# One layer of three mixers on one core: the order of all instructions from a list scheduler in the kernel, in place of an order written part by part

## The chip, the cores and the metric

The kernel runs on one NeuronCore of a Trainium2 chip. TensorE (PE in the profile) does the matrix products, VectorE (DVE), ScalarE (ACT) and GpSimd (POOL) the rest; all transfers are issued by SyncE (SP), in order. Each engine takes its instructions in the order of the program and waits for the others by semaphores. The metric is the device time of one execution in microseconds, less is better; three timed runs stand for the kernel before.

## The reference, cut to what matters

1040 tokens (16 learned ones and 1024 of the input) of 1024 channels in float32. They are normalised, projected once to 7832 columns, and three groups of heads work on their columns; the 2048 channels that come out are projected to 1024, normalised and added to the input.

```
hn   = rms_norm(h, norm_pre)
proj = hn @ w_in                                    # 1024 -> 7832
mixed = concat([gated_deltanet(p_a),                # 6 heads of 128
                rwkv7(p_b),                         # 8 heads of 64
                mamba2(p_c)])                       # 12 heads of 64, 4 groups
h    = h + rms_norm(mixed @ w_out, norm_post)       # 2048 -> 1024
```

DeltaNet and RWKV-7 carry a state from token to token through a matrix that differs for each token. In chunks (128 tokens for DeltaNet here, 64 for RWKV-7) this is a triangular system per chunk, and a short recurrence over the chunks. Mamba-2 has a scalar decay, so its chunks need no system.

## The kernel before, in words

**Tiles and products.** Channels lie on partitions, tokens along the free axis. `w_in` is cut in 61 tiles of 128 columns. A projection of one tile (`proj`, `conv`, `shifted`; tile name `pj`) has three pieces of about 347 tokens; a piece is 24 products on the whole 128x128 array into one bank: 8 tiles of the depth times three passes, because operands are split in a rounded part and its rest (type float32r). All else on TensorE is in plain float32, which takes two passes each, and much of it on smaller tiles of the array: 32x32, 64x64, 64x128, 128x64.

**Units.** The work is cut in units, written as generators that yield between their parts. `unit_a` is one DeltaNet head (a0 to a5): it projects k; makes the matrix of each chunk (`agk`); sends its blocks of 32 through DRAM to one block per partition; solves them there on VectorE (`solve32`, tile `alb`); merges blocks 32 to 64 to 128 (`am`); and goes over nine chunks (`aks`, `av`, `ads`, `aops`), each product waiting for an element-wise step on the one before. `unit_b` is a pair of RWKV-7 heads (b0 to b3), with grams (`bgr`), a solve (`blb`), merges (`bm`) and 17 chunks (`bsi`, `bu`, `bd`). `unit_c` is half of Mamba-2 (c0, c1). `unit_o` is the output projection (tile `po`): half of the columns for eight token tiles, two of them (po0 and po1) at once at the start, then the other half. Its weights come through a ring of three raw buffers (`or`), its input (`omre`, `omrw`) from DRAM.

**What sets the order.** `schedule` (L1169) takes units in the order of `PLAN` and keeps a clock of TensorE's work. `Meter` (L79) adds up about how long a part takes on TensorE, and how long the way back over the other engines is. When the next part of a scan should be ready on that clock it is emitted whole, otherwise one product of a projection. Emission gives a priority (`high_priority` with `PRI`, `EVA`, `CALM`), and the framework's own scheduler sets the order on each engine by priority and dependence. More than two units may scan at once, sharing two lanes of banks.

## Time and profile before

| what | value |
|---|---|
| three timed runs | 1523.97, 1532.54, 1538.36 us; median 1532.54 |
| span of the profiled execution | 1518.0 us (its own time beside the span is not shown) |
| instructions in the profile | 25931 |
| busy share PE, DVE, ACT, POOL | 94%, 67%, 43%, 16% |
| mean granted clock of TensorE | 0.970 |
| set-up; mixed middle; output projection | 0 to 38; 38 to 1302; 1302 to 1518 us |

A product of matrices shows from its start to its modelled end and overlaps with the next, so the pace is read from start to start. A float32 product leaves two records, one for each pass, and some records of products are missing from the trace. The granted clock is 1.0 at 2.4 GHz and 0.5 at 1.2 GHz. Counts of products and of changes between them are taken from the order of the program, times from the trace.

### The profile page before, as it was taken

Reading aid. Unit: us, or ns where it says so; the run is one execution under the profiler, and the core shown is the slowest. Engines: PE = TensorE matmul, PEld = TensorE weight load, DVE = VectorE, ACT = ScalarE, POOL = GpSimd, SP = SyncE. Lnnn points to the kernel's source line nnn. Section 1 sums busy time; section 2 is a strip of 40 time slices with the busy share of each in tenths; the row PEclk is TensorE's granted clock in tenths of the full one; section 3 lists DMA queues with packets and bytes.
Section 4 is the critical chain, followed back from the end, with each engine's and each line's share of the span. In section 5 each row is a group of like instructions: output and inputs, shape, how many; then the busy total and the mean of one; then the engine's idle time right before and its main releaser. Section 6 shows DMA issues by size and latency. Waiting matters only on the chain.

```text
span 1518.0 us, 25931 instructions
## 1 busy us (share of the span) xinstructions
PE 1427.0 (94%) x9657; PEld 1259.6 (83%) x9657; DVE 1014.6 (67%) x2688; ACT 647.8 (43%) x1814; POOL 239.2 (16%) x227
## 2 busy tenths in 40 slices
PE   4999999999999999997999999999999999889897
...
GB/s 187 58 85 43 70 33 39 29 41 64 29 30 47 49 74 43 86 31 53 46 43 50 43 46 53 36 29 57 97 59 61 43 36 44 169 159 89 250 193 56
DMA packets 102880, 104.28 MB, mean 69 GB/s; under 512 B 37915, under 2 KB 70427, under 8 KB 102755
## 3 DMA queue, kind: packets, MB, share of 16 engines
...
## 4 chain that ended last, share of the span: by engine, by line
PE 30%; DVE 14%; issue 5%; ACT 4%; DMA 3%; POOL 0%; SPq 0%; DVEq 0%; ACTq 0%; POOLq 0%
PE pj L96 14%; PE po L96 5%; DVE s_tmp L96 3%; DVE alb L96 2%; PE am L96 2%; DMA or<-in_w_out_dram 2%; PE bsi L96 1%; DVE aq L181 1%; DMA omrw<-d_mix 1%; PE aops L96 1%; PE ads L96 1%; DVE av L181 1%; PE aks L96 1%; PE av L96 1%; ACT clt L904 1%
## 5 line engine op out<-in xcount | busy, mean ns | idle before, releaser
L96 PE MATMUL pj<-hh,w 128*128 128x350 f32 (+8 forms) x2928 | 773.9, 338 | 0.2 <-ACT hh L261 0.2
L96 PEld LDWEIGHTS pj<-hh,w 128*128 128x128 f32 x2928 | 516.7, 192 | 13.2 <-issue 2.1
L96 PE MATMUL pj<-hl,w 128*128 128x350 f32 (+8 forms) x1464 | 493.4, 337 | 0.0
L150 POOL TENSOR_TENSOR w<-wr,w 128x512 fp32r<-128x512 f32 x122 | 173.6, 1424 | 870.3 <-ACT w L149 631.7
L96 PEld LDWEIGHTS pj<-hl,w 128*128 128x128 f32 x1464 | 281.3, 192 | 6.6 <-issue 0.9
L149 ACT CAST w<-wr 128x512 fp32r<-128x512 f32 x122 | 74.9, 615 | 75.8 <-PE pj L96 64.4
L96 PE MATMUL po<-ow,omw 128*128 128x512 f32 x408 | 95.5, 395 | 6.2 <-ACT omw L1064 3.7
L96 PEld LDWEIGHTS po<-ow,omw 128*128 128x128 f32 x408 | 77.2, 190 | 24.6 <-ACT omw L1064 4.4
L96 PE MATMUL po<-ow,ome 128*128 128x512 f32 x360 | 90.6, 399 | 4.6 <-ACT ow L1046 1.8
L96 PEld LDWEIGHTS po<-ow,ome 128*128 128x128 f32 x360 | 66.6, 188 | 20.1 <-POOL ow L1047 2.5
...
L96 DVE TENSOR_TENSOR buv<-bu,b_ib 64x128 f32<-64x128 f32 x68 | 19.1, 281 | 69.5 <-PE bu L96 69.3
...
L96 PEld LDWEIGHTS bsi<-buv,bgm 64*64 64x64 f32 (+1 forms) x528 | 42.1, 139 | 17.5 <-issue 2.2
L828 ACT COPY by<-bsi 64x128 f32<-64x128 f32 x64 | 16.7, 262 | 82.3 <-PE bsi L96 81.8
L181 DVE SCALAR_TENSOR_TENSOR cbc<-pj,pack,cbc 128x346 f32<-128x346 f32 (+4 forms) x72 | 40.5, 568 | 14.3 <-ACT cbc L178 13.5
...
L96 PE MATMUL bgr<-bar,bbk 64*128 64x128 f32 x272 | 43.8, 328 | 2.6 <-DVE bbk L96 2.0
L1065 DVE TENSOR_TENSOR ome<-omre,ome 128x512 fp32r<-128x512 f32 (+2 forms) x40 | 22.4, 594 | 34.1 <-ACT ome L1064 34.0
L1047 POOL TENSOR_TENSOR ow<-or,ow 128x512 fp32r<-128x512 f32 x16 | 21.0, 1316 | 135.9 <-ACT ow L1046 135.9
...
## 6 DMA issues: line engine op xcount, KB each, us to landing
wr<-in_wt_dram SPq DMA_DIRECT2D x122, 256.0 KB, 2.6
or<-in_w_out_dram SPq DMA_DIRECT2D x32, 256.0 KB, 2.6
omrw<-d_mix SPq DMA_DIRECT2D x32, 256.0 KB, 4.7
clt<-d_cs SPq DMA_DIRECT2D x24, 256.0 KB, 4.5
omre<-d_mix SPq DMA_DIRECT2D x24, 256.0 KB, 4.2
...
```

The source lines that it names most:

```text
L96: return op(out, *args, **kw)
L149: nc.scalar.copy(w[:, 0], raw)
L150: nc.gpsimd.tensor_tensor(w[:, 1], raw, w[:, 0].bitcast(F32), SUB)
L181: nc.vector.scalar_tensor_tensor(acc[:, a + z: b], p[:, o + z - s: o + b - a - s], cw[:, 3 - s: 4 - s], acc[:, a + z: b], MUL, ADD)
L828: nc.scalar.copy(yt[hs[(c - 1) % 2], (c - 1) // 2, :], pq[64:128, 0:128])
L904: nc.scalar.activation(t[:, e, i], t[:, e, i], AF.Exp, bias=self.ncs[:, 1 + 4 * w + i, k + e: k + e + 1])
L1047: (nc.vector if k % 2 else nc.gpsimd).tensor_tensor(t[:, 1], raw, t[:, 0].bitcast(F32), SUB)
L1065: nc.vector.tensor_tensor(t[:, 1], raw, t[:, 0].bitcast(F32), SUB)
```

## The change

The kernel's instructions stay as they are, and their order is set by the kernel itself. From `scalars` on, an engine call no longer emits: `write` records an `Instr` with the instructions it depends on (from the bytes that it reads and writes, and from buffers that come round again) and with a duration from a table. Each unit and each postponed projection is a `Task` with one queue per engine, so within a task an engine keeps the order of the source. The main loop takes, of all engines, the head that can start first by the table. On TensorE it keeps to projections until at least `BURST` (1.0 us) of them stand in a row, then takes scan parts in a round for as long as one is ready within `JOIN` (0.25 us), those of the bank that was last written first. On the other engines heads that are ready within 0.05 us are chosen by class (`LESS`). `emit` binds each instruction behind the one before on its engine, so the framework does not reorder. A lane of banks belongs to one unit at a time, so two units scan at once. `PLAN` is changed, and `Meter`, its constants and the waits that a part tells by its `yield` are gone.

```
-PLAN = "a0 b0 b1 b2 c0 b3 a1 a2 a3 c1 a4 a5"
+PLAN = "a0 b0 b1 a1 c0 b2 a2 c1 b3 a3 a4 a5"
-LOOK, LATE, EVAC, DMA = 0.05, 0.3, 2.0, 5.0
-PRI, EVA, CALM = 300, 700, 1500
+BURST, JOIN = 1.0, 0.25
+LESS = {"scan": 0.0, "ev": 0.3, "ld": 0.5, "calm": 1.0, "off": 0.4}
+AHEAD = 8
...
+            fast = name == "matmul" and args[0].dtype == F32R
+            i.mode = (r(rows), r(cols), fast)
+            i.step = (n / 2400 + 0.013 if fast else 0.109 if name == "transpose" else
+                      0.063 if r(cols) == 32 else 2 * max(0.058 if r(cols) == 64 else 0.112, n * 0.00085))
+            i.extra = {128: 0.165, 64: 0.108, 32: 0.07}[r(cols)]
+        elif key == "DVE":
+            i.step = 0.065 + n * (0.00116 if len(ins) > 2 else 0.00105)
+        elif key == "ACT":
+            i.step = 0.105 + 0.00078 * n if name == "copy" else 0.14 + 0.00086 * n
+        elif key == "POOL":
+            i.step = 0.04 + n * (0.0024 if name == "tensor_tensor" else 0.001)
+        else:
+            last = min(a.ap[-1][1] if a.ap[-1][0] == 1 else 1 for a in (out, args[0]))
+            total = int(np.prod(out.shape)) * 4
+            i.step, i.extra = 0.46, total / 380e3 * (1 if last >= 128 else 1.5 if last >= 32 else 4)
+        self.task.q[key].append(i)
...
+    def ready(self, i):
+
+        if i.start is None:
+            t = 0.0
+            for d in i.deps:
+                if d.done is None:
+                    return None
+                if not d.eng == i.eng == "PE":
+                    t = max(t, d.done + SEES[i.eng])
+            i.start = t
+        return i.start
+
+    def emit(self, i, start):
+        r = i.go()
+        ins, was = r.ins, self.before.get(i.eng)
+        if was is None:
+            self.tc.keep_in_program_order(r)
+        else:
+            self.tc.add_manual_dep(ins, was, mybir.DependencyInfo(mybir.DependencyClass.NoSync, mybir.DependencyReason.DATA), reason="order")
+        self.before[i.eng] = ins.name
+        if i.eng == "PE":
+            if self.array and self.array != i.mode:
+                if self.array[:2] != i.mode[:2]:
+                    start += 0.093
+                if i.mode[2] and not self.array[2]:
+                    i.step += 0.1
+            self.array = i.mode
+        self.free[i.eng] = start + i.step
+        if i.eng == "SP":
+            self.bus = max(self.bus, start + 0.4) + i.extra
+            i.done = max(start + 2.0, self.bus + 1.3)
+        else:
+            i.done = start + i.step + i.extra
+        i.start, i.go = start, None
+        i.deps = ()
+        i.task.q[i.eng].pop(0)
...
-            if ready and (when(ready[0]) <= self.clock + LOOK or not can):
-                s = ready[0]
-                self.clock = max(self.clock, when(s))
-                if s["lane"] is None:
-                    used = [sum(o["lane"] == g for o in active) for g in range(len(GB))]
-                    s["lane"] = used.index(min(used))
-                self.lane = s["lane"]
-                with self.tc.high_priority(CALM if s["calm"] else PRI):
-                    step(s)
...
+                    if s["on"] and not s["on"]["done"] or not safe(s):
+                        continue
+                    if s["lane"] is None:
+                        open_ = [g for g in range(len(GB)) if all(o["lane"] != g for o in active)]
+                        if not open_:
+                            continue
+                        s["lane"] = open_[0]
...
+        while True:
+            advance()
+            best = None
+            for e in ENGINES:
+                heads = []
+                for t in self.tasks:
+                    if t.q[e]:
+                        i = t.q[e][0]
+                        r = self.ready(i)
+                        if r is not None:
+                            heads.append((max(r, self.free[e]), r, i))
+                if not heads:
+                    continue
+                if e == "PE":
+                    now = self.free["PE"]
+                    pj = min((h for h in heads if h[2].cls == "pj"), key=lambda h: h[0], default=None)
+                    sc = [h for h in heads if h[2].cls != "pj"]
+                    sc = min(sc, key=lambda h: (h[0] > now + 0.02 if h[2].out == last else 1, h[0]), default=None)
+                    if pj is None or sc is None:
+                        pick = sc or pj
+                    elif round_:
+                        pick = sc if sc[0] <= max(now + JOIN, pj[0]) else pj
+                    else:
+                        pick = sc if since >= BURST and sc[0] <= max(now + 0.03, pj[0]) or sc[0] < pj[0] - 0.3 else pj
+                else:
+                    first = min(h[0] for h in heads)
+                    pick = min((h for h in heads if h[0] <= first + 0.05), key=lambda h: h[1] + LESS[h[2].cls])
+                if best is None or pick[0] < best[0]:
+                    best = pick
+            if best is None:
```

Three places in the order. First TensorE in the scan of b0 over its chunks: `bsi`, `bu` and `bd` are the products of one chunk, `pj` those of a projection. Before, around chunk 10:

```order
L96 MATMUL bsi_10_3060<-b_s,bar_1_1201 128x128
L96 MATMUL bsi_10_3060<-buv_1_2275,bgm_01_1452 64x64
L96 MATMUL bsi_10_3060<-buv_1_2275,bgm_11_1454 64x64
L96 MATMUL pj_1_3183<-hh,w_1_2950 128x386
L96 MATMUL pj_1_3183<-hl,w_1_2950 128x386
L96 MATMUL pj_1_3183<-hh,w_1_2950 128x386
L96 MATMUL bu_10_3077<-b_x,bgm_01_1452 64x64
L96 MATMUL bu_10_3077<-b_x,bgm_11_1454 64x64
L96 MATMUL pj_2_3253<-hh,w_0_2945 128x322
L96 MATMUL pj_2_3253<-hl,w_0_2945 128x322
L96 MATMUL pj_2_3253<-hh,w_0_2945 128x322 x2
L96 MATMUL bd_10_3086<-buv_1_2275,bbt_1_1587 128x128
```

Now, at chunk 13 of the same unit:

```order
L205 MATMUL bsi_13_2898<-b_s,bar_1_1104 128x128
L205 MATMUL bsi_13_2898<-buv_1_1958,bgm_01_1253 64x64
L205 MATMUL bsi_13_2898<-buv_1_1958,bgm_11_1255 64x64
L205 MATMUL pj_1_2919<-hh,w_0_2653 128x346 x2
L205 MATMUL pj_1_2919<-hl,w_0_2653 128x346
L205 MATMUL pj_1_2919<-hh,w_0_2653 128x346 x2
L205 MATMUL pj_1_2919<-hl,w_0_2653 128x346
L205 MATMUL pj_1_2919<-hh,w_0_2653 128x346
L205 MATMUL bu_13_2940<-b_x,bgm_01_1253 64x64
L205 MATMUL bu_13_2940<-b_x,bgm_11_1255 64x64
L205 MATMUL pj_1_2919<-hh,w_0_2653 128x346
```

Three and four projections stood between two parts of the scan; now there are seven.

Second, TensorE where the blocks of b0 are merged (`bm`, on 32x32 tiles). Before, beside the grams of b1 (`bgr`, 64 rows by 128 columns of the array):

```order
L96 MATMUL bm_9_2497<-bgm_01_1452,bdd_2411 32x32
L96 MATMUL bm_17_2508<-bdd_2411,bgm_10_1453 32x32
L96 MATMUL bgr_11_2544<-bar_0_2267,bbk_0_2269 128x128
L96 MATMUL bm_9_2497<-bgm_01_1452,bdd_2411 32x32
L96 MATMUL bm_17_2508<-bdd_2411,bgm_10_1453 32x32
L96 MATMUL bgr_11_2544<-bar_0_2267,bbk_0_2269 128x128
L96 MATMUL bm_17_2508<-bdd_2411,bgm_10_1453 32x32
L96 MATMUL bgr_01_2526<-bar_0_2267,bbk_0_2269 128x128
L96 MATMUL bm_9_2497<-bgm_01_1452,bdd_2411 32x32
L96 MATMUL bgr_11_2544<-bar_0_2267,bbk_0_2269 128x128
L96 MATMUL bm_17_2508<-bdd_2411,bgm_10_1453 32x32 x2
```

Now, beside the chunks of a0 (`aks`, `av`, `ads`, `aops`, on the whole array):

```order
L205 MATMUL bm_0_2076<-bdd_2075,bgm_00_1252 32x32 x9
L205 MATMUL aks_3_2096<-a_s,ak_457 128x128
L205 MATMUL bm_0_2111<-bgm_00_1252,bdd_2075 32x32 x9
L205 MATMUL av_3_2113<-a_x,alo_654 128x128
L205 MATMUL bm_9_2127<-bdd_2075,bgm_01_1253 32x32 x8
L205 MATMUL ads_3_2129<-a_vn,akd_657 128x128
L205 MATMUL aops_3_2131<-a_s,aq_957 128x128
L205 MATMUL aops_3_2131<-a_vn,aup_653 128x128
L205 MATMUL bm_9_2142<-bgm_01_1253,bdd_2075 32x32 x8
L205 MATMUL aks_4_2148<-a_s,ak_457 128x128
L205 MATMUL bm_17_2159<-bdd_2075,bgm_10_1254 32x32 x9
L205 MATMUL av_4_2162<-a_x,alo_654 128x128
```

The products of a bank stood one by one among those of two other banks; now the eight or nine of a bank follow each other.

Third, the transfers on SP at the start of the output projection (`or` is a raw weight, `omre` an input, those with 136 and the next higher numbers belonging to po1). Before:

```order
L1062 DMA omre_0_13501<-d_mix 128x4x128
L1062 DMA omre_4_13506<-d_mix 128x128
L1043 DMA or_3_13532<-in_w_out_dram 128x512
L1062 DMA omre_6_13511<-d_mix 128x2x128
L1043 DMA or_4_13537<-in_w_out_dram 128x512
L1043 DMA or_6_13542<-in_w_out_dram 128x512
L1062 DMA omre_0_13592<-d_mix 128x4x128
L1062 DMA omre_8_13516<-d_mix 128x4x128
L1043 DMA or_7_13547<-in_w_out_dram 128x512
L1043 DMA or_8_13552<-in_w_out_dram 128x512
L1036 DMA d_mix<-cz_11846 128x1024
L1036 DMA d_mix<-cz_11847 128x1024
```

Now:

```order
L205 DMA or_8_13527<-in_w_out_dram 128x512
L205 DMA or_9_13529<-in_w_out_dram 128x512
L205 DMA or_10_13531<-in_w_out_dram 128x512
L205 DMA or_11_13533<-in_w_out_dram 128x512
L205 DMA or_12_13535<-in_w_out_dram 128x512
L205 DMA or_13_13537<-in_w_out_dram 128x512
L205 DMA or_14_13539<-in_w_out_dram 128x512
L205 DMA or_15_13541<-in_w_out_dram 128x512
L205 DMA omre_0_13543<-d_mix 128x4x128
L205 DMA omre_4_13545<-d_mix 128x128
L205 DMA omre_6_13547<-d_mix 128x2x128
L205 DMA omre_8_13549<-d_mix 128x4x128
```

The first piece of po1's input (`omre_0_13592` before, `omre_0_13543` now) stood behind three of the twelve weights of the ring, and stands behind all of them. On TensorE, before:

```order
L96 MATMUL ads_5_13465<-a_vn,akd_11511 128x128
L96 MATMUL aops_5_13469<-a_s,aq_12107 128x128
L96 MATMUL aops_5_13469<-a_vn,aup_11489 128x128
L96 MATMUL po_13617<-ow_11_13569,ome_8_13518 128x512
L96 MATMUL aks_6_13479<-a_s,ak_11201 128x128
L96 MATMUL po_13617<-ow_11_13569,ome_8_13518 128x512
L96 MATMUL po_13618<-ow_0_13488,ome_0_13594 128x512 x2
L96 MATMUL av_6_13622<-a_x,alo_11490 128x128
L96 MATMUL po_13617<-ow_12_13574,ome_12_13523 128x512 x2
```

Now:

```order
L205 MATMUL aops_8_13633<-a_s,aq_12439 128x128
L205 MATMUL aops_8_13633<-a_vn,aup_12236 128x128
L205 MATMUL po_13554<-ow_0_13378,ome_0_13544 128x512 x2
L205 MATMUL aoT_0_13663<-pack,avt_12982 128x128 x4
L205 MATMUL aoT_1_13664<-pack,avt_12982 128x128 x4
L205 MATMUL po_13554<-ow_0_13378,ome_0_13544 128x512
L205 MATMUL po_13553<-ow_1_13380,ome_0_13384 128x512 x3
L205 MATMUL po_13554<-ow_1_13380,ome_0_13544 128x512 x3
```

po0 (`po_13617`) went through its weights up to the twelfth before po1 (`po_13618`) began; now po1 (`po_13554`) takes its first weight before po0 (`po_13553`) its second, and the rest of a5's chunks stands ahead of both.

## Rows read from the trace of the kernel before

**Rows 1.** The page, part 1: engine, busy us, share of the span, instructions.

```profile
PE 1427.0 (94%) x9657; PEld 1259.6 (83%) x9657; DVE 1014.6 (67%) x2688; ACT 647.8 (43%) x1814; POOL 239.2 (16%) x227
```

**Rows 2.** Stages: start:end, length, busy us of each engine (instructions), clock, DMA.

```profile
0.00:38.00 38.00, 17.02 (x92) 14.62 (x92) 27.48 (x73) 21.68 (x41) 10.38 (x16) 1.00 0.52 187
38.00:1302.00 1264.00, 1216.04 (x8701) 1089.92 (x8700) 879.88 (x2344) 548.68 (x1598) 210.43 (x197) 0.97 0.17 49
1302.00:1344.00 42.00, 35.38 (x186) 26.64 (x186) 25.78 (x67) 22.27 (x61) 10.51 (x8) 1.00 0.68 214
...
1405.00:1445.00 40.00, 33.75 (x137) 26.06 (x136) 22.51 (x38) 21.87 (x41) 5.37 (x4) 0.96 0.80 237
```

**Rows 3.** Timeline, PE, projections: start us, length, engine, line, operation, tiles, shape, count.

```profile
700.11 0.32 PE L96 MATMUL pj<-hl,w 128*128 128x350 f32 x1
700.27 0.49 PE L96 MATMUL pj<-hh,w 128*128 128x350 f32 x2
```

**Rows 4.** Timeline, PE, a stretch of products on 64x64 tiles.

```profile
385.82 0.55 PE L96 MATMUL bn<-pack,bbk 128*64 128x2 f32 x7
...
386.56 0.32 PE L96 MATMUL pj<-hh,w 128*128 128x348 f32 x1
386.81 0.44 PE L96 MATMUL bu<-b_x,bgm 64*64 64x64 f32 x4
387.18 0.43 PE L96 MATMUL pj<-hh,w 128*128 128x350 f32 x1
387.45 0.32 PE L96 MATMUL pj<-hl,w 128*128 128x350 f32 x1
```

**Rows 5.** Timeline, PE, a stretch of products on the whole array.

```profile
1128.83 0.32 PE L96 MATMUL pj<-hh,w 128*128 128x348 f32 x1
1129.04 0.89 PE L96 MATMUL cds<-ctmp,cbt 128*128 128x192 f32 x4
1129.63 0.46 PE L96 MATMUL pj<-hh,w 128*128 128x348 f32 x1
1129.92 0.32 PE L96 MATMUL pj<-hl,w 128*128 128x348 f32 x1
```

**Rows 6.** Stages of granted clock 0.50: two of ten, and the sum of all.

```profile
251.85:279.16 27.31, 27.31 (x139) 21.16 (x139) 9.49 (x19) 3.70 (x10) 0.00 (x0) 0.50 0.04 7
...
893.56:896.97 3.41, 3.41 (x13) 3.41 (x13) 3.41 (x10) 0.46 (x1) 0.00 (x0) 0.50 0.00 0
...
sum 88.74, PE 84.09 PEld 70.49 DVE 41.57 ACT 19.70 POOL 1.82; mean PE 8.41 PEld 7.05 DVE 4.16 ACT 1.97 POOL 0.18
```

**Rows 7.** Timeline, PE, ahead of the longest of them.

```profile
249.22 0.48 PE L96 MATMUL bgr<-bar,bbk 64*128 64x128 f32 x2
249.63 0.24 PE L96 MATMUL bm<-bgm,bdd 32*32 32x32 f32 x2
```

**Rows 8.** Waits of PE: who waited for what, us in total, times, longest.

```profile
PE avT L96 <- DVE av L184: 11.7, 5, 9.6
```

**Rows 9.** Timeline, one chunk of a unit "a".

```profile
1241.11 0.30 PEld L96 LDWEIGHTS aks<-a_s,ak 128*128 128x128 f32 x2
...
1242.22 0.38 PE L96 MATMUL av<-a_x,alo 128*128 128x128 f32 x2
...
1243.06 0.30 PEld L96 LDWEIGHTS ads<-a_vn,akd 128*128 128x128 f32 x2 [0.27 <-ACT a_vn L96]
...
1243.99 0.30 PEld L96 LDWEIGHTS aks<-a_s,ak 128*128 128x128 f32 x2
```

**Rows 10.** Timeline, SP: first and last of eight rows with twelve weights.

```profile
1302.40 0.33 SPq L1043 DMA_DIRECT2D or<-in_w_out_dram  x1
...
1325.24 0.33 SPq L1043 DMA_DIRECT2D or<-in_w_out_dram  x1
```

**Rows 11.** The page, part 6: issues, KB each, median us to landing.

```profile
omre<-d_mix SPq DMA_DIRECT2D x24, 256.0 KB, 4.2
```

**Rows 12.** Groups on DVE by shape: one operation of a projection's evacuation, mean ns.

```profile
L181 DVE SCALAR_TENSOR_TENSOR cx<-pj,pack,cx 128x346 f32<-128x346 f32 x42 | 23.6, 571 | 9.1 <-ACT cx L178 8.5
```

355 lines of the change are left out of this document (245 added, 110 removed).

## The prediction

> **What bounds the kernel now.** First the busy share of each engine, then the same by stage. TensorE is busy for 1427.0 us of the span of 1518.0 [rows 1], so all its idle time together is 91.0 us. By stage [rows 2] that is 21.0 us in the set-up (0 to 38 us), 48.0 us in the long middle (38 to 1302 us) where projections and scans are mixed, 6.6 us at the start of the output projection (1302 to 1344) and 6.2 us around the second half of its columns (1405 to 1445). Idle time is therefore not the main stock. The second thing to see is that "busy" is not "at its pace". In a run of projection products the next starts 0.16 us after the one before, though each lasts 0.32 us [rows 3]; what makes that step longer is lost without showing as idle. Two things do.
>
> One is the change of kind. Between two projection products 0.89 us apart stand four products on a 64x64 tile [rows 4]. Two projection steps are 0.32. The small ones cost 0.06 to 0.08 each: seven products on a 128x64 tile take 0.55 us with the tail of the last (0.08 each), and less without it; I take 0.06, so 0.24 for four. What is left, 0.33 us (0.25 at 0.08), went into going to the small tile and coming back. Where the scan's products use the whole 128x128 array, the same reckoning is [rows 5]: 1.09 us, less 0.32, less four products of 192 columns. Between the first one's start and that of the next projection lie 0.59 us, 0.15 each, and with the last one's tail 0.89, which less a tail of 0.13 to 0.3 is 0.15 to 0.19 each. That leaves 0.01 to 0.18 us; I take 0.06.
>
> The other is the clock. In ten stretches, 88.7 us together, the granted clock was 0.50, which is 1.2 GHz instead of 2.4 [rows 6]. The longest, 27.3 us, follows a place where products on 64x128 and 32x32 tiles alternate two by two with hardly a projection among them [rows 7]; another begins after an idle time. In the stretch at 893.6 us TensorE did 13 products in 3.41 us, where 0.16 us each would be 2.1, so 1.3 us of 3.4 was lost. At that share the ten lose 34 us; half of all of it, 44 us, is the most they can lose.
>
> **The change, part by part.** No instruction is added or removed: 7758 matrix products, 480 transfers and the same VectorE and ScalarE operations stand in both programs. All that moves is order, and the units' plan.
>
> *Switches.* Counting the order, a stretch of scan products between projections occurs 564 times before and 379 times now. Stretches that touch another tile than 128x128 fall from 287 to 206: 81 x 0.33 = 27 us less. Those on the whole array fall from 277 to 173: 104 x 0.06 = 6 us less (1 to 19). The stretches that are left are longer and hold 17 more changes of tile beyond the two of entering and leaving; at half of 0.33 us each that is 3 us back. Sum: -30 us, between -18 (81 x 0.25, and 1, less 3) and -43. I take -28, since some changes lie in waits and cost nothing of their own.
>
> The Trainium skill, TensorEngine Tiling (Array Packing), section Key Properties, says that changing the tiling mode drains TensorE, and names no cost for going between the data types on the same tile. By that rule only tile changes pay; the order has 740 of them before and 595 now, and 145 x 0.165 us would be -24 us. The rows of the two kinds of stretch (0.33 against 0.01 to 0.18) agree with it, and it lies within the bounds.
>
> *Clock.* Of the 34 us, the stretch of 27.3 us (10 to 12 us of loss) belongs to the two-by-two alternation [rows 7]. That goes: the new order finishes one bank before it takes another, and puts seven projections behind a round. But the rounds are longer. In the new order 22 stretches without projections exceed 3 us of work against 9 before, and those that are mostly 32x32 products (merging the triangular blocks of a unit "a", 48 of them in one stretch) are what preceded low clock before. I expect eight to twelve short dips at 1.3 to 1.7 us each, 13 to 18 us, in place of 34: I take -14, between -28 and +5.
>
> *Waits in the middle.* The 48.0 us are waits of a part that stands in the order before its input is there; the longest is 9.6 us for VectorE [rows 8]. The new scheduler places a scan product only when, by its own table of durations, the input is ready, and a projection otherwise. Are seven projections long enough to hide a step of a scan? 7 x 0.16 = 1.12 us, with a switch 1.2 to 1.4 us. A chunk of a unit "a" at its quickest takes 2.88 us over three such steps [rows 9], 0.96 us each on average, the product itself included. So each step has about 0.2 to 0.4 us to spare. I take -20: a good half goes, since two places have no projections to spare (units a1 and b1 scan together through a stretch of 67 products, because the tiles of c0 do not fit before they end) and since real durations spread about the table. Bounds: -40 and +10.
>
> *The start of the output projection.* This gets worse. The two first token tiles, po0 and po1, take each weight in turn, now strictly: po1's first product stands behind po0's first three, and po1's input is now loaded after twelve weights on the one transfer queue (SP), where before its first piece stood among them and po0 ran on alone with whatever weight had come. Before, twelve weights were issued between 1302.40 and 1325.24 us, 1.9 us each with other transfers among them [rows 10]. Twelve by themselves take 11 us at twice that pace, an estimate, and 23 at the same; then po1's input takes 4.2 us to land [rows 11], and its split comes on top. So po1 starts 17 to 28 us after the last projection. TensorE has to set against it the rest of unit a5's scan, three chunks of 2.88 us and some transposes, 10 to 12 us. That leaves 5 to 17 us of waiting where 6.6 us stand now: +6 us, between 0 and +12. All behind it (the second half's 6.2 us, the end) stays.
>
> *Not touched.* The set-up's 21.0 us, and the number of instructions. VectorE and ScalarE do the same work; they were not what TensorE waited for except at the waits counted above.
>
> Sum: -28 - 14 - 20 + 6 = -56, so a span of 1462 us where 1518.0 was. The profiled execution shows its span alone; the three timed runs have a median of 1532.5, 14.5 above it (1524.0 to 1538.4). Taken from the median: **1476 us**, 3.7% less. All low ends together would be a span of 1407, all high ends 1527; ends seldom meet, and this case's own range is 1455 to 1505 us of time.
>
> **Rivals.**
> *A. A frozen order that waits (slower).* Each engine now holds one order for the whole middle, made from a table. If a VectorE or ScalarE operation of a scan stands behind an evacuation of a projection whose input comes later than the table says, TensorE waits at the next round, and no projection can step in. The price of one such miss is the time of one evacuation operation, 0.57 us [rows 12]. It decides at 56 us over 379 rounds, 0.15 us per round, which is one round in four. At one in two it is 379 x 0.28 = 108 us, and the time 1584; at one in three 72 us, 1548. The Trainium skill, TensorE: Matmul & The Clock Gate, section Architectural detail, speaks for this rival: it calls the queues of VectorE and ScalarE strictly first in, first out. No row here tests it; if it holds, the miss costs what the row on the evacuation says. Against it stands the spare time of 0.2 to 0.4 us per step, and that the order before was frozen as well and yet waited only 48 us. One in three or worse: 0.10. Between one in six and one in three, which gives 1512 to 1548, no change by and large: 0.13.
> *B. The gain is larger.* The switches near their full price (-38), hardly a dip left (-28), nearly all waits gone (-40), the output as reckoned (+6): -100, 1432 us. For it: projections are there to the very end, since the last scan ends 7 us of work behind the last projection in the new order. Against it: the long stretches of 32x32 products. 0.15.
> *C. Fewer switches, no less time.* If the time in the switches was time in which the scan had to wait anyway, removing them brings back the wait, and of the 28 us nothing is left: 1504 us. For it: stretches on the whole array show prices near zero at times. Against it: 0.33 us was paid with no idle time beside it [rows 4]. 0.10.
> The forecast keeps 0.52.
>
> **How the numbers follow.** A measurement of this kernel can tell about 1% from no change, 15 us: faster means below 1517, slower above 1548. The forecast, B and C lie below 1517 nearly whole (0.52, 0.15, and 0.07 of C's 0.10), with 0.03 of A's milder half: 0.77. Slower is A's strong half but for 0.01 near its edge, 0.09. The rest, 0.14, is no change. The range for 8 in 10 leaves out the better half of B below (0.07) and A's strong half with a little of its milder one above (0.13): 1434 to 1532.
>
> **What the profile of the changed kernel would show.** Switches: about 380 stretches of projections, most of seven products, and the 0.33 us unchanged at a 64x64 stretch. Clock: fewer and shorter stretches at 0.50, sum 35 to 50 us, at the merges of units "a"; if it is over 80, that term is wrong. Waits: 20 to 35 us of idle time in the middle; over 70, in many waits under 0.6 us for VectorE, is rival A. Output: one wait of 5 to 17 us before po1's first product, released by ScalarE's or VectorE's work on its input. The forecast is wrong if the stretch from 38 us to the first output product shrinks by less than 40 us.

## The result, and the profile after

The changed kernel takes **1654.98 us** (median of three, 1650.3 to 1655.37) where the kernel before takes 1532.54: the ratio is 1.0805, with a 95% interval from 1.0745 to 1.0866. The forecast was 1476 us, so the sign was wrong. The profiled executions have spans of 1648.5 and 1518.0 us, a difference of 130.5. Of the runs in the table of experiments, two of the four of e10 (1649.1 and 1652.5 us) lie over 1.5% above its quickest, and its time and ratio leave them out.

The busy share of the engines after, from the first part of the page (engine, busy us, share of the span, instructions), to be read against [rows 1], and the row of the granted clock from its second part (40 equal slices, tenths):

```profile
PE 1471.1 (89%) x9657; PEld 1314.6 (80%) x9657; DVE 1035.5 (63%) x2688; ACT 649.1 (39%) x1814; POOL 232.2 (14%) x227
...
PEclk9899979999989999999979999999979788798998
```

The same instructions keep TensorE busy 44.1 us longer (1471.1 against 1427.0), and it is idle for 177.4 us instead of 91.0. Idle time and slower work grew together. The table by stage says where; its columns are those of [rows 2]:

```profile
0.00:38.00 38.00, 19.02 (x96) 16.59 (x97) 25.99 (x69) 20.69 (x38) 7.78 (x14) 1.00 0.42 156
38.00:1399.90 1361.90, 1251.72 (x8754) 1139.10 (x8753) 908.01 (x2372) 555.60 (x1624) 206.18 (x199) 0.93 0.16 48
1399.90:1442.00 42.10, 29.91 (x118) 23.79 (x118) 16.06 (x40) 13.52 (x34) 7.85 (x6) 0.72 0.41 128
1502.00:1548.00 46.00, 32.50 (x133) 25.65 (x131) 15.24 (x22) 18.35 (x31) 10.44 (x8) 0.88 0.48 155
1548.00:1648.00 100.00, 79.16 (x306) 61.41 (x306) 54.22 (x155) 23.53 (x52) 0.00 (x0) 0.89 0.41 132
```

The middle (38 us to the first output product) is 1361.9 us long, 97.7 more than before; the output projection behind it 248.6, 32.8 more. The set-up's idle time is 19.0 instead of 21.0.

Stages of granted clock 0.50, three of thirty and the sum, against [rows 6]:

```profile
686.88:693.71 6.83, 3.36 (x13) 3.36 (x14) 6.49 (x19) 1.33 (x6) 0.00 (x0) 0.50 0.00 0
...
850.72:871.20 20.48, 20.48 (x151) 18.36 (x147) 4.97 (x10) 5.37 (x12) 0.00 (x0) 0.50 0.01 2
...
1403.68:1427.57 23.89, 13.99 (x44) 10.72 (x45) 15.37 (x39) 12.95 (x33) 7.85 (x6) 0.50 0.46 143
...
sum 238.92, PE 205.67 PEld 181.75 DVE 128.30 ACT 77.36 POOL 29.01; mean PE 6.86 PEld 6.06 DVE 4.28 ACT 2.58 POOL 0.97
```

238.9 us at 1.2 GHz, where 88.7 stood. Some of these stages are full of work (the second: 20.48 of 20.48 busy), some lie around a wait (the other two); the second, too, begins right behind a wait, as shown below.

The waits of TensorE after, longest lists first (who waited for what, us in total, times, longest), against [rows 8]:

```profile
PE czT L205 <- DVE ctmp L205: 11.5, 2, 5.9
...
PE akT L205 <- ACT akT L205: 10.8, 4, 5.1
PE po L205 <- ACT po L205: 10.3, 6, 1.9
PE am L205 <- DVE add L205: 9.7, 5, 3.1
```

No single place carries it. In the middle there are 35 waits of 1 us or more, 83.1 us together (10 and 25.0 before), while those of 0.3 to 1 us are as before: 34 with 18.8 us, against 32 with 18.1.

One of the long ones, on TensorE (timeline, columns as [rows 3], in brackets the idle time before and who ended it):

```profile
684.28 0.47 PE L205 MATMUL pj<-hh,w 128*128 128x336 f32 x2
690.35 0.90 PE L205 MATMUL czT<-pack,cz 128*128 128x128 f32 x3 [5.59 <-DVE ctmp L205]
690.91 0.63 PE L205 MATMUL pj<-hl,w 128*128 128x336 f32 x1
```

The projection that goes on at 690.91 is the piece that stopped at 684.28, with the same operands. It could have run through the wait, but stands behind `czT` in the order. What VectorE did meanwhile:

```profile
669.08 0.19 DVE L205 TENSOR_TENSOR s_tmp<-blb 68x30 f32<-68x30 f32 x1 [9.77 <-DMA blb<-d_l]
...
670.65 1.23 DVE L205 TENSOR_TENSOR s_tmp<-blb 68x108 f32<-68x108 f32 x1
671.91 1.24 DVE L205 TENSOR_TENSOR blb<-blb,s_tmp 68x108 f32<-68x108 f32 x1
673.18 0.29 DVE L205 TENSOR_TENSOR s_tmp<-blb 68x130 f32<-68x130 f32 x1
...
675.25 1.39 DVE L205 TENSOR_TENSOR s_tmp<-blb 68x184 f32<-68x184 f32 x1
...
677.05 1.34 DVE L205 TENSOR_TENSOR s_tmp<-blb 68x198 f32<-68x198 f32 x1
...
689.47 0.36 DVE L205 TENSOR_TENSOR blb<-blb,s_tmp 68x198 f32<-68x198 f32 x1
689.75 0.54 DVE L205 SCALAR_TENSOR_TENSOR ctmp<-ctmp,czT 128x384 f32<-128x384 f32 x1
```

and ScalarE and GpSimd:

```profile
683.39 0.50 ACT L205 ACTIVATE ctmp<-czT 128x384 f32<-128x384 f32 x1
...
670.48 2.54 POOL L205 TENSOR_TENSOR w<-wr,w 128x512 fp32r<-128x512 f32 x2 [1.22 <-ACT w L205]
675.14 1.29 POOL L205 TENSOR_TENSOR w<-wr,w 128x512 fp32r<-128x512 f32 x1 [2.12 <-ACT w L205]
676.76 1.41 POOL L205 TENSOR_TENSOR w<-wr,w 128x512 fp32r<-128x512 f32 x1 [0.33 <-ACT w L205]
```

The input of `ctmp` is there at 683.89, when ScalarE's operation ends. VectorE comes to it at 689.75, since operations of a solve (`blb`) stand ahead and it runs them without a gap: VectorE is behind its place in the order. Four of the solve's operations took 1.23 to 1.39 us where those around them take 0.29 to 0.36, each beside a weight split (`w<-wr,w`) of GpSimd; that is 3.9 us of the 5.9 by which VectorE is late. Where the other 2 us come from is not shown. VectorE had stood idle for 9.77 us until the transfer of the solve's blocks landed (669.08), so a transfer later than in the table is one candidate. The clock falls in the wait, at 686.88, and stays down until 693.71.

Such waits for a transfer are new on the two engines (waits of VectorE and of ScalarE, after):

```profile
ACT w L205 <- DMA wr<-in_wt_dram: 43.3, 15, 8.2
DVE s_tmp L205 <- DMA blb<-d_l: 23.4, 3, 10.9
```

Before, ScalarE waited 0.3 us for projections' weights (`wr`), and VectorE never for blocks that a solve was to begin with. The operations of all units that stand behind such a wait in the frozen order wait with it. How much of TensorE's idle time that makes is not shown, and no experiment here changes the durations of transfers in the table.

The long stage of full work begins so:

```profile
850.38 1.44 PE L205 MATMUL am<-add,alo 32*32 32x32 f32 x31 [2.81 <-DVE add L205]
...
852.62 0.95 PE L205 MATMUL pj<-hh,w 128*128 128x346 f32 x2
...
856.59 1.97 PE L205 MATMUL am<-add,alo 64*64 64x64 f32 x16
...
858.94 0.49 PE L205 MATMUL pj<-hl,w 128*128 128x344 f32 x1
859.23 0.78 PE L205 MATMUL pj<-hh,w 128*128 128x344 f32 x2
```

After a wait of 2.81 us come two rows of merges, with seven projections between them (852.62 to 854.94). The granted clock falls at 850.72, 0.34 us into the first row, and the projections behind the second still start 0.29 us apart (858.94 to 859.23) instead of 0.16.

Stretches of over 3 us from one product of the projections' kind (float32r) to the next number 40 in the middle, 258 us together; before there were 20, 103 us. The waits lie partly in them (68.0 us of the 258), but most of it is work: 1750 records of scan products, against 632. The longest, 19.2 us from 478.3, holds 134 records of products and 0.2 us of idle time: two units feed each other, and the rule that takes scan parts as long as one is ready within `JOIN` never stops. But the granted clock is 1.00 all through this one (478.3 to 497.4 us), so a long row of scan products is not by itself what lowers it.

The price of a switch is as it was [rows 4]:

```profile
252.96 0.32 PE L205 MATMUL pj<-hh,w 128*128 128x350 f32 x1
253.21 0.44 PE L205 MATMUL bu<-b_x,bgm 64*64 64x64 f32 x4
253.58 0.42 PE L205 MATMUL pj<-hh,w 128*128 128x350 f32 x1
253.84 0.32 PE L205 MATMUL pj<-hl,w 128*128 128x350 f32 x1
```

0.88 us from the projection before to the second behind, where 0.89 stood.

And the second half of the output projection, where nothing was expected:

```profile
1518.16 0.80 PE L205 MATMUL po<-ow,omw 128*128 128x512 f32 x1 [9.46 <-ACT ow L205]
...
1547.93 1.62 PE L205 MATMUL po<-ow,omw 128*128 128x512 f32 x3 [3.49 <-DVE ob L205]
...
1580.64 13.49 PE L205 MATMUL po<-ow,omw 128*128 128x512 f32 x51 [1.90 <-ACT po L205]
```

One wait of 9.46 us for a weight, one of 3.49 for the evacuation of the bank, and some 1.9 us ahead of each token tile, six times. On VectorE the order shows why:

```profile
1560.67 1.48 DVE L205 TENSOR_TENSOR omw<-omrw,omw 128x512 fp32r<-128x512 f32 x2 [0.74 <-ACT omw L205]
1562.06 0.68 DVE L205 TENSOR_TENSOR ob<-ob,po 128x512 f32<-128x512 f32 x1
```

Inputs of a later token tile (`omw`, waiting for transfers) are split ahead of the evacuation of this one (`ob<-ob,po`). Loads and evacuations belong to one task, and within a task an engine keeps the order of the source.

### The profile page after: what moved, and what is told of

The parts are those of the page before. It is cut to its first block, busy times and chain, and to the rows that moved or that the text cites. A ratio compares the mean times of both kernels' runs of the same rounds, so it can differ in the third digit from the quotient of the medians.

```text
span 1648.5 us, 26009 instructions
## 1 busy us (share of the span) xinstructions
PE 1471.1 (89%) x9657; PEld 1314.6 (80%) x9657; DVE 1035.5 (63%) x2688; ACT 649.1 (39%) x1814; POOL 232.2 (14%) x227
## 3 DMA queue, kind: packets, MB, share of 16 engines
q8 instruction: 76, 1.25, 0.3%
## 4 chain that ended last, share of the span: by engine, by line
PE 45%; DVE 27%; ACT 9%; DMA 8%; issue 7%; SPq 2%; POOL 1%; DVEq 0%; ACTq 0%; POOLq 0%
PE pj L205 22%; PE po L205 6%; DVE s_tmp L205 4%; PE bsi L205 3%; PE am L205 2%; DVE alb L205 2%; SPq L205 2%; DMA omrw<-d_mix 2%; DVE blb L205 2%; DMA or<-in_w_out_dram 1%; DVE clt L205 1%; DMA wr<-in_wt_dram 1%; DVE cbc L205 1%; PE bgr L205 1%; DVE bgm L205 1%
## 5 line engine op out<-in xcount | busy, mean ns | idle before, releaser
L205 PE MATMUL pj<-hh,w 128*128 128x350 f32 (+8 forms) x2880 | 763.6, 342 | 3.5 <-ACT w L205 1.9
L205 PEld LDWEIGHTS pj<-hh,w 128*128 128x128 f32 x2880 | 527.4, 199 | 16.0 <-issue 3.0
L205 POOL TENSOR_TENSOR w<-wr,w 128x512 fp32r<-128x512 f32 x120 | 165.8, 1399 | 925.7 <-ACT w L205 828.0
L205 PE MATMUL po<-ow,omw 128*128 128x512 f32 x408 | 105.0, 419 | 26.8 <-ACT po L205 10.3
L205 PEld LDWEIGHTS po<-ow,omw 128*128 128x128 f32 x408 | 81.8, 203 | 50.0 <-ACT po L205 13.2
L205 PE MATMUL po<-ow,ome 128*128 128x512 f32 x360 | 84.6, 396 | 6.7 <-ACT ome L205 6.7
L205 ACT CAST w<-wr 128x512 fp32r<-128x512 f32 x120 | 69.9, 615 | 43.8 <-DMA wr<-in_wt_dram 43.3
L205 DVE TENSOR_TENSOR s_tmp<-blb 68x30 f32<-68x30 f32 (+14 forms) x120 | 48.6, 405 | 26.3 <-DMA blb<-d_l 23.4
L205 DVE SCALAR_TENSOR_TENSOR cbc<-pj,pack,cbc 128x346 f32<-128x346 f32 (+4 forms) x72 | 40.9, 568 | 21.3 <-ACT cbc L205 20.6
L205 DVE TENSOR_TENSOR omw<-omrw,omw 128x512 fp32r<-128x512 f32 x32 | 21.9, 691 | 46.7 <-ACT omw L205 46.5
L205 DVE SCALAR_TENSOR_TENSOR b_s<-bd,b_wc,b_s 64x64 f32<-64x64 f32 x120 | 33.8, 282 | 22.9 <-PE bd L205 21.3
L205 DVE SCALAR_TENSOR_TENSOR cx<-pj,pack,cx 128x346 f32<-128x346 f32 (+2 forms) x54 | 31.2, 577 | 18.6 <-ACT cx L205 17.4
```

Of the source, the lines that this page charges most:

```text
L205: i.go, i.eng, i.cls, i.task, i.done, i.start = (lambda: op(out, *args, **kw)), key, self.cls, self.task, None, None
```

## The experiments

Three causes were in question at first: the durations in the table (T), rounds of scan parts without end (R), and in the output projection the written order within one task (Q); behind them the plan of units, small misses at each step, and the recursions that fill VectorE's queue. All times are medians, ratios are to runs of the kernel before on the same chip. The other columns are worked out from the trace of each profiled execution: idle time of TensorE in the middle; us of the middle at 1.2 GHz (number of stages) and what the products that start in them take beyond their pace at full clock (changes of kind included, so it can pass half of the first number); sum of the stretches in the middle of over 3 us without a product of the projections' kind; and the length from the first output product to the end.

| run | time (range) | ratio (95%) | idle | at 1.2 GHz; cost | without projection | output |
|---|---|---|---|---|---|---|
| before | 1532.5 | 1 | 48.0 | 85 (9); 44.5 | 103 | 215.8 |
| after | 1655.0 | 1.081 (1.075-1.087) | 110.2 | 188 (24); 87.8 | 258 | 248.6 |
| e1_table | 1615.7 (1610.0-1620.3) | 1.057 (1.051-1.063) | 87.3 | 205 (18); 96.8 | 306 | 247.0 |
| e2_cap | 1666.9 (1661.1-1677.0) | 1.092 (1.086-1.098) | 117.0 | 212 (21); 97.2 | 141 | 249.5 |
| e3_oldplan | 1679.7 (1672.3-1685.9) | 1.099 (1.094-1.105) | 124.1 | 266 (27); 124.6 | 320 | 249.4 |
| e4_margin | 1653.3 (1648.0-1655.8) | 1.082 (1.077-1.086) | 112.1 | 219 (20); 101.6 | 243 | 244.0 |
| e5_out | 1627.6 (1616.7-1636.7) | 1.061 (1.054-1.068) | 107.9 | 174 (21); 79.6 | 253 | 222.7 |
| e6_burst | 1581.5 (1578.6-1585.7) | 1.032 (1.028-1.037) | 79.4 | 160 (19); 76.7 | 247 | 222.4 |
| e7_warm | 1604.5 (1593.9-1606.8) | 1.045 (1.040-1.050) | 85.7 | 143 (14); 65.7 | 138 | 226.1 |
| e8_rec_after | 1609.3 (1606.9-1610.9) | 1.051 (1.046-1.056) | 81.4 | 157 (18); 77.1 | 202 | 246.8 |
| e9_rec_before | 1503.5 (1499.2-1506.9) | 0.982 (0.977-0.986) | 26.8 | 99 (11); 55.3 | 108 | 212.1 |
| e10_thin_after | 1624.3 (1620.1-1628.4); trace of 1652.5 | 1.061 (1.053-1.068) | 96.9 | 440 (22); 236.2 | 420 | 249.4 |
| e11_plan | 1577.5 (1575.5-1582.3) | 1.030 (1.024-1.035) | 76.9 | 174 (21); 84.8 | 193 | 220.2 |
| e12_filler | 1613.8 (1611.0-1620.4) | 1.052 (1.049-1.055) | 75.7 | 116 (17); 52.1 | 69 | 225.8 |
| e13_tight_before | 1621.4 (1619.1-1623.5) | 1.060 (1.054-1.066) | 110.5 | 242 (18); 98.8 | 236 | 203.2 |
| e14_slack | 1681.5 (1674.8-1689.9) | 1.101 (1.093-1.109) | 148.5 | 304 (21); 122.5 | 392 | 219.0 |
| e15_allow08 | 1522.5 (1512.3-1527.0) | 0.993 (0.990-0.997) | 50.7 | 109 (13); 51.6 | 95 | 205.7 |
| e16_allow12 | 1557.3 (1553.9-1560.1) | 1.017 (1.012-1.021) | 84.2 | 119 (9); 42.3 | 126 | 223.8 |
| e17_late045 | 1565.5 (1553.4-1568.5) | 1.021 (1.015-1.026) | 87.6 | 121 (12); 37.9 | 113 | 215.2 |
| e18_allow06 | 1564.3 (1559.9-1572.9) | 1.021 (1.016-1.027) | 66.2 | 156 (10); 70.9 | 159 | 209.5 |

**e1_table: the table of durations set right.** VectorE on small tiles of PSUM, prefix sums and ScalarE's sums over a row get their measured durations, and a VectorE operation with two SBUF inputs that falls into a GpSimd operation starts at its end.

```
+            if psum and n <= 128:
+                i.step = 0.285 if n <= 64 else 0.258
+            if name == "tensor_tensor_scan":
+                i.step = 0.065 + n * 0.002
...
+            if "accum_out" in kw:
+                i.step += 0.16
...
+        if i.eng == "DVE" and i.mode and self.port[0] <= start < self.port[1]:
+            start = self.port[1]
```

> The scheduler's table is corrected from the trace of the change: VectorE steps that read PSUM on small tiles, the scan, ScalarE's sums over a row, and a VectorE operation with two SBUF inputs that meets a long GpSimd operation ends only after it. Theory T (the waits come from durations that are too short in the table): TensorE's idle time between 38 us and the first output product falls from 110 to 50 or 60 us and the time from 1655 to about 1600. Rival F (a fixed order waits whatever the table says): idle stays at 95 to 125 us and the time within 1% of 1655.

39 us less than after, and 22.9 us less idle time in the middle: between what T and F expected, nearer to F in the idle time. Wrong durations are one cause, worth about a third of the loss. One reservation: an edit of the scheduler changes the whole order, and e15 to e18 show that small changes of one number alone move the time by -8 to +35 us. The rest of the waits stays, those of ScalarE for weights (37.8 us) and of VectorE for a solve's blocks (30.5 us) among them.

**e2_cap: rounds of scan parts limited.** A projection is put in after 1.2 us of scan work.

```
+                    elif round_ and spent > 1.2 and pj[0] <= now + 0.1:
+                        pick = pj
```

> A round of scan products is ended after 1.2 us of work if a projection is ready. Theory R (the half clock follows long rounds of scan products, above all the merges of units a): the stretches at half clock fall from 245 us together to 130 or less, and the time to about 1615, in spite of some 60 more switches (20 us at most). Rival W (the half clock follows the waits): the stretches stay at 210 to 270 us and the time at 1655 to 1675.

No gain (12 us worse). The rounds are cut (141 us without projections instead of 258), and most of the low stages at the merges of units "a" are gone, but others come at the merges of units "b". One stretch of 48.2 us from 1120.4 has 291 records of scan products and no projection; that its projections had been spent earlier is likely, not shown. Rival W came out, in the clock and in the time: over the whole run 264 us are at 1.2 GHz, and 19 of the 21 stages in the middle begin behind a wait of TensorE (counted as below, under Clock).

**e3_oldplan: the units in the old order.**

```
-PLAN = "a0 b0 b1 a1 c0 b2 a2 c1 b3 a3 a4 a5"
+PLAN = "a0 b0 b1 b2 c0 b3 a1 a2 a3 c1 a4 a5"
```

> The new scheduler with the old order of the units (b1, b2 and b3 early, the units a late). Theory P (the new order of units leaves too little beside the scans): the waits in the middle fall from 110 to under 80 us and the time to 1600 or less. Rivals T and F: the plan is not the cause, the time stays within 1.5% of 1655.

25 us worse than after, with more idle time (124.1). The new plan is not the cause; with this scheduler it is the better of the two.

**e4_margin: 0.4 us of margin ahead of every TensorE product that waits for another engine.**

```
-                    t = max(t, d.done + SEES[i.eng])
+                    t = max(t, d.done + SEES[i.eng] + (0.4 if i.eng == "PE" else 0.0))
```

> The scheduler takes every input of TensorE from another engine as ready 0.4 us later than its table says, so a product is placed later behind projections. Theory T: the shortest waits, those under 0.4 us and 0.4 us of each longer one (some 75 of them), go, 25 to 35 us less time: about 1625. Rival B (backlogs of several us on VectorE and ScalarE): the waits of 1 to 6 us, which make up most of the sum, stay, and the time changes by less than 1%.

No change, as rival B expected. If many small misses made the waits, 0.4 us would have taken them; the waits of 1 us and over still sum up to 74.7 us (83.1 after).

**e5_out: loads of the output projection in a task of their own.**

```
+        with self.of(self.fetch, "ld"):
+            return self.o_weight_(n, k, ahead)
...
+        with self.of(self.fetch, "ld"):
+            return self.o_mixed_(m, ks, name, ahead)
```

> The change as it is, but in the output projection the loads and splits of inputs and weights are a task of their own for the scheduler, so that on VectorE and ScalarE the sums of one token tile no longer stand behind the splits for the tile two further on. Theory Q (within one task the scheduler keeps the written order on each engine, and that holds up the second half of the columns): the stretch from the first output product to the end falls from 249 us to about 225 and the time by 15 to 25 us, to about 1632; the waits of 1.9 us for ScalarE's po before each token tile go. Rival D (the loads themselves are late): the stretch stays within 5 us of 249.

27 us less; the output of the profiled execution is 25.9 us shorter (248.6 to 222.7), as expected. TensorE there, in the timeline of its second half:

```profile
1531.22 26.21 PE L205 MATMUL po<-ow,omw 128*128 128x512 f32 x102 [2.12 <-ACT po L205]
1557.85 11.85 PE L205 MATMUL po<-ow,omw 128*128 128x512 f32 x51 [0.41 <-ACT po L205]
```

The waits ahead of a token tile are shorter, and 102 products in a row take 26.2 us. Shown: the written order within one task was most of the loss there, 25.9 of 32.8 us.

**e6_burst: the table and the output of e1 and e5, and `BURST` 0.5.**

```
-BURST, JOIN = 1.0, 0.25
+BURST, JOIN = 0.5, 0.25
```

> The corrected table of e1, the output tasks of e5, and half the projections between two rounds (0.5 us instead of 1.0). Theory K (long bursts and long rounds are what costs: the half clock and the waits): time 1616 - 20 - 20 = about 1575, with more stretches (450 or more). Rival S (the switches are what costs, as the change assumes): the gain of e1 and e5 alone, about 1596, plus some 100 more switches at 0.2 to 0.33 us, 1616 to 1630.

1581.5 us, 73 less than after. e1 and e5 alone gave 39 and 27, 66 together, so little is left for the shorter row of projections (some 400 stretches, not the 450 expected). Of the runs here that keep the rule, e11 alone is quicker, by 4 us. Of the 58.9 us by which its span (1576.9) still exceeds the one before, 31 are idle time in the middle, 32 are at half clock, 7 in the output, and -11 in all else.

**e7_warm: on top of e6, a scan product is put off when the last 4 us held less than 1.4 us of projections.**

```
+                    elif pj[0] <= now + 0.1 and sum(p[1] for p in past) < 1.4:
+                        pick = pj
```

> As e6, and a scan product is put off while the last 4 us held under 1.4 us of projections and one is ready. Theory R2 (the half clock follows stretches with few projections in them, whether waits or scan rounds fill the rest): stretches at half clock fall from 258 us (e1) to 150 or less, the time to 1560 or less. Rival N (there are places where no projection is ready at all, since the next unit's tiles do not fit, and there the rule can do nothing): they stay above 200 us, and the time at 1580 to 1610.

The clock does better (cost 65.7 instead of 76.7) and the time is 23 us longer, within what rival N expected; over the whole run 182 us are at 1.2 GHz, between the two forecasts. The profiled executions differ by 11.5 us in the middle: clock -11, idle time +6, and 17 in full-clock work with 97 more switches. So what the clock gives is spent elsewhere, on switches as far as this reckoning tells.

**e8_rec_after and e9_rec_before: the solve's recursion stops after 6 of 30 steps, in either kernel.**

```
-        for j in range(1, 31):
+        for j in range(1, 7):
```

> The change with 24 of the 30 steps of each triangular recursion left out (480 of VectorE's dependent operations, some 190 us of its 1035; the blocks are then not solved). Theory V (TensorE waits for short steps that stand behind such recursions on VectorE, and part of the half clock comes from these waits): idle time in the middle falls from 110 to 60 us or less, the stretches at half clock from 245 to 190 or less, the time by 70 us or more, to 1585 or less. Rival G (VectorE's load is not the point): the time falls by less than 25 us.

> The same 24 of 30 recursion steps left out of the kernel before. Theory V for the change alone (the order before put these waits under projections): the time falls by less than 25 us, its waits in the middle are 48 us in all. Rival: the recursion costs the kernel before as much as the changed one, 70 us or more.

Without 480 of VectorE's operations, the changed kernel gains 46 us and the one before 29. Between the two 106 us remain of 122: the recursions delay VectorE's queue, but they are not the main part of what the change lost. Both times lie between the two forecasts of their run, and the idle time of the change falls to 81.4 us, not to 60.

**e10_thin_after: the third product of each projection step on 64 columns.** 1440 products lose 283 of some 347 columns each; at n/2400 us for n columns, as the kernel's own table has it, that would be 170 us of TensorE's work.

```
-                        self.engines[2].matmul(p[:, : b - a0], w[kt // 4][:, x, kt % 4, :], h[:, kt, a0:b],
+                        self.engines[2].matmul(p[:, : b - a0 if m < 2 else 64], w[kt // 4][:, x, kt % 4, :], h[:, kt, a0:b if m < 2 else a0 + 64],
```

> The change with the third product of every projection step cut to 64 columns (the low part of the weights is then left out for most tokens). It takes 1440 x 0.12 = 170 us of work from TensorE and leaves every other engine its work. Theory E (TensorE's work is still the bound): the time falls by 150 us or more, to 1505 or less. Theory L (the chain of the two scans through VectorE, ScalarE and the transfers is as long as TensorE's work, and less work beside it means more waits and more half clock): the time falls by 40 to 110 us, idle in the middle rises above 150 us and the half clock above 300 us.

The edit does not take 170 us. Three products of a projection step in its trace, the second row being the thin one and the next full one:

```profile
720.13 0.32 PE L205 MATMUL pj<-hl,w 128*128 128x346 f32 x1
720.29 0.43 PE L205 MATMUL pj<-hh,w 128*128 128x64 f32 x2
720.56 0.32 PE L205 MATMUL pj<-hl,w 128*128 128x346 f32 x1
```

From one `hl` product to the next, three products on, are 0.43 us where the trace of the change has 0.48: what the thin product saves comes back in part at the product behind it. 1440 times 0.05 us is some 70 us, an estimate from these rows, so theory E's 150 us could not come, and the run does not decide it. The two runs at 1620 and 1628 us are 27 to 35 us quicker than after, with mean clocks of 0.875 and 0.867 over the run where the change has 0.922 to 0.926. The profiled execution is one of the two long ones (1652.5 us, mean clock 0.850); its row of the granted clock:

```profile
PEclk9899975698965899999978999955678777798899
```

and in the middle's stage:

```profile
38.00:1401.40 1363.40, 1266.52 (x8724) 1153.29 (x8723) 897.61 (x2364) 548.83 (x1613) 209.16 (x199) 0.84 0.16 48
```

The mean clock of the middle is 0.84 instead of 0.93, 440 us are at half clock, and idle time even fell (96.9), against theory L. The clock falls about as often as in the change (22 stages against 24) and stays down longer (20 us each against 7.8). So less dense work between the scan products went with a lower clock, in the two quick runs by their mean clock and in this execution by its stages.

**e11_plan: on top of e6, another plan,** `a0 b0 a1 c0 b1 b2 a2 c1 b3 a3 a4 a5`.

```
-PLAN = "a0 b0 b1 a1 c0 b2 a2 c1 b3 a3 a4 a5"
+PLAN = "a0 b0 a1 c0 b1 b2 a2 c1 b3 a3 a4 a5"
```

> The kernel of e6 with the units in the order a0 b0 a1 c0 b1 b2 a2 c1 b3 a3 a4 a5. Theory M (the order of units sets where no projection is left beside two scans): its order has 81 us of scan products in stretches of over 3 us against 107 in e6, so some 15 to 25 us less half clock and waits, about 1560. Rival: within 1% of e6's 1581.

4 us less than e6, within the spread of either, as the rival expected: this other meeting of the units does not bring back what is left.

**e12_filler: on top of e7, products of no use where no projection is ready.** 150 of them, 128x512 on the whole array, in a bank of the projections.

```
+    def heat(self):
+        p = self.pp.tile([128, 512], F32, tag="proj", name="heat")
+        with self.of(self.hot, "pj"):
+            for m in range(5):
...
```

> The kernel of e7, and where its scheduler finds no projection ready and few in the last 4 us, five useless 128x512 products of the projections' kind are put in (150 in all, 150 x 0.21 = 32 us of TensorE's work; nothing reads them). Theory R2 (the half clock follows places with few products of that kind, not the small tiles or the changes of kind as such): the stretches at half clock fall from 182 us (e7) to 120 or less, and what the fillers cost comes back: time 1585 to 1610, against 1604. Rival Z (the half clock follows the scan's products themselves): half clock stays above 165 us and the time rises by 25 us or more.

9 us more than e7, 4 us above what was expected. Half clock falls from 143 to 116 us and its cost by 13.6; idle time falls by 10.0. The filler itself, 150 at 0.26 us (the pace in e5's rows), is 39 us, an estimate. So dense work in bare places raised the clock, but bought with useless products it doesn't pay. The fillers also stand in places that were waits, so this does not tell whether the waits or the rows of small products had held the clock down.

**e13_tight_before: the kernel before, with too little allowance for the way back.** Its planner takes the time of the other engines times `SLOW` plus `LATE`.

```
-LOOK, LATE, EVAC, DMA = 0.05, 0.3, 2.0, 5.0
+LOOK, LATE, EVAC, DMA = 0.05, 0.0, 2.0, 5.0
-SLOW = 1.0
+SLOW = 0.6
```

> The kernel before with the time that it allows for a scan step's way through the other engines cut to 0.6 of it, and without the 0.3 us on top. Theory A2 (the order before waits little because it allows each step more time than it takes): idle in the middle rises from 48 to 75 us or more, the time by 20 us or more, to 1552 or more. Rival: the allowance is not what counts, the time stays within 1% of 1532.

The old scheduler with a hopeful estimate lands at 1621 us, with the idle time of the change (110.5 against 110.2) and more half clock (242 us). A unit "b" in its timeline:

```profile
464.15 0.77 PE L96 MATMUL bsi<-b_s,bar 128*128 128x128 f32 x2 [0.41 <-ACT by L828]
...
465.94 0.68 PE L96 MATMUL bu<-b_x,bgm 64*64 64x64 f32 x4 [0.40 <-ACT b_x L96]
467.00 0.80 PE L96 MATMUL bd<-buv,bbt 128*128 128x128 f32 x2 [0.38 <-DVE buv L96]
...
468.77 0.80 PE L96 MATMUL bsi<-b_s,bar 128*128 128x128 f32 x2 [0.35 <-ACT by L828]
```

The scan runs chunk after chunk, 55.6 us without a projection (452.1 to 507.7), and waits 0.4 us at each step, where the planner held the next part for ready. At half clock a chunk takes 4.62 us (464.15 to 468.77). Parts placed before their input is there reproduce waits and half clock together, in a kernel without the change.

**e14_slack: on top of e6, VectorE's and ScalarE's durations in the table times 1.25.**

```
+        if key in ("DVE", "ACT"):
+            i.step *= 1.25
```

> The kernel of e6 with every VectorE and ScalarE step in the scheduler's table 1.25 times as long. Theory A2: the products are placed later behind projections, idle in the middle falls from 79 to 50 us or less, the time from 1581 to 1565 or less. Rival L (the scans' chain is as long as TensorE's work, so a scan that is put off is missing at the end, where no projection is left): time 1600 or more.

100 us worse than e6, as rival L expected. Slack doesn't mend it: 392 us pass in stretches without a projection. That the scans, longer by the table, come late and projections run out is L's reason, and fits.

**e15_allow08, e16_allow12, e17_late045, e18_allow06: the kernel before with other allowances.**

```
-SLOW = 1.0
+SLOW = 0.8
```

(e16: `SLOW` 1.2; e17: `LATE` 0.45; e18: `SLOW` 0.6 with `LATE` 0.3.)

> The kernel before with 0.8 of its allowance and the 0.3 us on top left: between e13 (0.6 and 0) and the kernel before. Theory A2: time between 1545 and 1590, idle in the middle 60 to 90 us. Rival (e13 was a chance order, the allowance has no steady effect): within 1% of 1532.

> The kernel before with 1.2 times its allowance. Theory A2 (waits are what the allowance saves): idle in the middle falls below 40 us, time 1505 to 1525, faster than both. Rival L (a longer allowance makes the scans late, and projections run out at their end): 1540 or more.

> The kernel before with 0.45 us on top of each step instead of 0.3. Theory A2: idle in the middle falls below 45 us, time 1515 to 1530. Rival L: 1540 or more.

> The kernel before with 0.6 of its allowance, the 0.3 us on top left: half of e13's edit. Theory A2' (below some length the step's real time is longer than the allowance, and the waits begin): 1560 to 1620, idle in the middle above 80 us. Rival (it was the 0.3 us on top that e13 missed, without which a scan follows itself at once): within 1.5% of 1531.

A bowl: 0.6 gives 1564 us, 0.8 1522.5, 1.0 about 1531, 1.2 1557, and `LATE` 0.45 1565.5. The kernel before stands near the bottom. But a longer allowance saved no waits: idle time rises on both sides (66.2 at 0.6; 84.2 at 1.2; 87.6 with `LATE` 0.45), against what theory A2 expected of e16 and e17, and e15 kept its time where A2 expected 1545 or more. That any reshuffled order costs some 2% by chance is a rival that these runs do not exclude; e13, at 6%, is beyond it. e15 is 0.7% faster than the kernel before (ten runs) and the fastest here that does all of the work. Its middle:

```profile
38.00:1315.10 1277.10, 1226.41 (x8799) 1100.57 (x8800) 891.02 (x2377) 552.58 (x1632) 208.09 (x197) 0.96 0.17 50
```

In this one execution the middle is longer than before [rows 2] and the output 10 us shorter, so 0.7% is shown only as a whole.

## Why the prediction was wrong

By its terms, in spans; the forecast was -56:

| term | forecast | measured |
|---|---|---|
| switches | -28 | -13 |
| clock, in the middle | -14 | +43 |
| waits in the middle | -20 | +62 |
| output projection | +6 | +33 |

With 53 more of the products' records before the first output product (some 5 us) these make up the 130.5. The switches' term is all that work at full clock took beyond its pace, 130.2 before and 116.9 after. The profiled execution of the change took 1.8 us more than its span; the 14.5 us that the prediction put between span and time was mostly a quick execution before, not a cost.

**The step that failed** is this one: "The new scheduler places a scan product only when, by its own table of durations, the input is ready, and a projection otherwise", with 0.2 to 0.4 us to spare per step. The comparison was of a chunk at its quickest with a row of projections. In place of 28 us of waits there were 110.2. Readiness by the table is readiness only if VectorE, ScalarE and the transfers keep to it, and each engine has one frozen queue for all units. Operations that took longer than the table has them put everything behind them back. VectorE was 5.9 us late at `ctmp`, and spare time of 0.4 us is nothing to that (e4). Of 105 us of waiting for a scan product, in some 93 the next projection in the order, mostly one to four products further on, had all its inputs; this comes from the trace and the dependences of the program. Mending the table (e1) takes 22.9 us of the idle time and 39 us of the time. The old scheduler, made hopeful in the same way (e13), has the same idle time, 110.5 us. So the step failed, and its reason is shown for those 22.9 us. Why some 39 of the 62 us of added waits stay in e1 is open. Also, the -20 was called a good half of 48.0, and is 42% of it.

**Rival A** had this mechanism and was given 0.10 in its strong half. Its price was wrong: one evacuation, 0.57 us, in one round of two to four. Of its sign, over 70 us of idle time came, but not the many waits under 0.6 us: there were no more of 0.3 to 1 us than before, and 25 more of 1 us and over. A late queue costs its whole backlog, seldom, not one operation, often. The Trainium skill, TensorE: Matmul & The Clock Gate, section Architectural detail, calls the queues of VectorE and ScalarE strictly first in, first out; this trace agrees, with an operation whose input was there at 683.89 and that ran at 689.75.

**Clock.** The 22 long stretches without projections were seen ahead and valued as short dips of 1.3 to 1.7 us each. The mark for a wrong term was over 80 us at half clock; it is 239. The prediction looked for the low clock at rows of small products alone. What TensorE did just ahead of each fall of the clock in the middle says more (a fall counts as behind a wait when TensorE was idle for 1 us or more in the 5 us ahead; the bounds are a choice made for this count):

| the clock falls behind | before | after |
|---|---|---|
| products only | 7 stages, 71.7 us | 7 stages, 54.6 us |
| a wait | 2 stages, 13.7 us | 13 stages, 71.7 us |
| a wait and merges on 32x32 tiles | none | 4 stages, 61.4 us |

The part that was forecast to shrink did shrink, by 17 us. What came on top, 119 us, begins behind waits, those of the failed step. That the waits lowered the clock is what the order of events suggests; no run takes the waits away alone. Long stretches without a projection go with the low clock as well: 103 us in such stretches and 85 at half clock before, 258 and 188 after, in e14 392 and 304. But e2 has 141 and 212, nearly all of it behind waits, and the longest stretch of the change ran at full clock.

**Switches.** Right in kind: 369 stretches in the middle where 380 were counted, at the old price. The gain is half as large, and the price was mis-sized: what the changes of kind took in the middle fell from 56.5 to 41.6 us, while at 0.33 and 0.06 us for the 287 and 277 stretches they would have taken 111 us before. The 0.33 us is right where it was read [rows 4] and too much for the mean.

**Output.** The wait of `po1` is there as forecast: 5.5 us, released by ScalarE's work on its input, and idle time in that stage is 12.2 against 6.6, +5.6. That this meets the +6 is luck: 6.6 us of it are waits inside the rest of a5's scan, which was reckoned without any. "All behind it stays" failed: the second half lost 20.6 us to idle time, and had 27 us at 1.2 GHz where 3.4 stood, since the written order within a task was not looked at beyond the start. e5 shows it for most of the loss.

**Still open.** Some 50 us stand between e6 and the kernel before, idle time and half clock in equal parts. The old rule emits a scan part with an allowance and otherwise projections one by one, 529 stretches; e7 came near to that number (497) without its result. Which part of the old rule makes its evenness was not found. Two differences stand untested. One is the transfers in the table: in e6 ScalarE still waits 32.0 us for weights and VectorE 27.6 us for a solve's blocks. The other is the number of units that scan: two at once now, more than two before.
